# Three chains in PSUM for layer 1's up units, and eight copies behind the last square

## The chip, the cores and the metric

The kernel runs on one core of one Trainium2 chip. The metric is the device time of one execution in microseconds. Five engines work side by side: TensorE (PE) multiplies matrices into the eight banks of PSUM; VectorE (DVE), ScalarE (ACT) and GpSimd (POOL) work elementwise; SyncE (SP) issues DMA transfers. Each engine runs its own instructions in order and waits for the others through semaphores.

## What is computed

A decoder trunk of two layers over 512 tokens of width 1024: layer 0 is a convolution module and a SwiGLU FFN, layer 1 is windowed attention and a SwiGLU FFN, with a final norm. The change lies in the FFN of layer 1, where attention has just been added to h:

```python
def rmsnorm(x, g):
    xf = xf * lax.rsqrt(jnp.mean(xf * xf, axis=-1, keepdims=True) + EPS)
    return xf * g

def swiglu_ffn(x, w_up, w_down):
    gate, up = jnp.split(x @ w_up, 2, axis=-1)
    return (jax.nn.silu(gate) * up) @ w_down

h = h + attn @ w_o[j]
h = h + swiglu_ffn(rmsnorm(h, norm_ffn[l]), ffn_w_up[l], ffn_w_down[l])
return rmsnorm(h, norm_final)
```

The hidden width is 2816.

## The kernel before

**Split products.** All weights and activations in this part are fp32 split into a high and a low part, and each product is three matmuls: high x high, high x low, low x high (`mm3`, lines 356 to 358). Weights come in chunks of 128 x 1024 from DRAM (`load`, line 248, SP's queue, into four buffers). `split_weights` makes the high part on ACT (a cast, line 273) and the low part on DVE (line 276); both have four buffers, and the split runs three chunks ahead of PE.

**The up product in pairs.** The 2816 hidden columns are worked in eleven pairs (0 to 10) of 256 gate and 256 up columns. Pairs 0, 2, 4, 7 and 10 are plain (`plain_pair`): 96 matmuls of 512 columns in four banks. The pairs in `SEVENS` (1, 3, 5, 6, 8, 9), here called units, use a scheme of seven block products in place of eight (`seven_pair`): the weights are cut into A11, A12, A21, A22, the activations into B11 to B22, and besides plain blocks there are sums S1 to S4 of weight blocks and T1 to T4 of activation blocks. A block is 24 matmuls of 256 columns into one bank. The S sums are made beforehand by DMAs that add in DRAM (`prepare`, lines 264 and 268, on SP's and POOL's queues).

Before the change every block of a unit has a bank of its own, seven a unit. The elementwise engines put the results together in four gate tiles c11 to c22: ACT copies A11 (line 787) and S1 (789); when S2 is done DVE adds it to c11 (791) and combines it with S3 (792), POOL adds and subtracts (793, 794); A12, S4 and A22 are added or subtracted by DVE (796, 798, 800). The order of the blocks in a unit is A11, S3, S1, S2, A12, S4, A22, and in unit 1 A11, S1, S3, S2, A12, S4, A22. Afterwards the gate is scaled (806, DVE), passed through silu (807, ACT) and multiplied (808, POOL), and `forms_of` makes the T sums of the result (822, POOL) and splits them (lines 515 to 519, ACT and DVE) for the down product.

**The down product** (`low_pairs`, line 848) takes two pairs at a time, also in seven blocks, in the order A11, S1, S2, A12, S3, S4, A22, and adds several blocks up in PSUM in three chains x, y, z, two banks each, given by `CHAINS` (chain, and where the result goes):

```python
    CHAINS = {"A11": ("x", 0, 0), "S1": ("z", 1, 1), "S2": ("x", 0, 1), "A12": ("y", 0, 0), "S3": ("x", 1, 1),
              "S4": ("z", 0, 1), "A22": ("x", 1, 0)}
```

DVE reads a chain after each block (857); A12 goes through ACT and POOL (854, 855). The order of the stages is up 0, 1, 2, low 0, then up p, up p+1, low p-1 for p = 3, 5, 7, 9.

**The seam.** Attention's output product ends with eight tiles of h, one after another. For each tile DVE adds it to h (line 1410), and `Rows.on_h` makes the scaled high part on ACT (`split_scaled`, line 510) and the low part on DVE (511), squares the tile on ACT (463) and adds the squares on DVE (467). Their sum goes through eight one-column products (477), a power on POOL (481) and a product (503) to the scale of the rows. `Rows.sums` makes the activation's T blocks for the units: eight copies of h scaled by the gain on ACT (726), four subtractions or additions on POOL (732), then splits (515 to 519). It is stepped from inside pair 0. In unit 1, between blocks, PE also transposes h by four products (`flip`, 1425) and ACT copies the result (1426).

**Order.** The program is written in one order, but a planner with its own time estimates puts each engine's instructions in the order in which they are issued: a ready instruction is taken before one that would wait. PSUM banks come from a pool of eight. `tc.issue_after(x)` forces an instruction behind x on x's engine.

Of the kernel before, what the change touches and what calls it, by code (L numbers as in the profile page):

```python
# [14 lines left out]
ALU = mybir.AluOpType  # L15
# [37 lines left out]

SEVEN = ("A11 B11", "S3 T3", "S1 T1", "S2 T2", "A12 B21", "S4 B22", "A22 T4")
SEVENS = (1, 3, 5, 6, 8, 9)
SEVEN_FIRST = ("A11 B11", "S1 T1", "S3 T3", "S2 T2", "A12 B21", "S4 B22", "A22 T4")
SEVEN_LOW = ("A11 B11", "S1 T1", "S2 T2", "A12 B21", "S3 T3", "S4 B22", "A22 T4")


def by_seven(layer, pair):
    return layer == 1 and pair in SEVENS


def order_of(kind, pair):
    if kind == "low":
        return SEVEN_LOW
    return SEVEN_FIRST if pair == SEVENS[0] else SEVEN


def ups(layer, pair):
# [4 lines left out]


def blocks_of(kind, pair):
    return [(kind, pair, n.split()[0]) for n in order_of(kind, pair)]  # L80


def is_block(c):
# [3 lines left out]
def chunk_plan():  # L87
# [28 lines left out]
    for kind, pair in STEPS1:  # L116
        plan.extend(blocks_of(kind, pair) if kind == "low" or by_seven(1, pair) else ups(1, pair))
# [82 lines left out]
def hybrid_trunk(ctx: ExitStack, tc: tile.TileContext, xT, W, prm_in, wdw_in, sinks, relb, onehot, fin, lead, out):  # L200
    nc = tc.nc
# [10 lines left out]
    def uid(s):  # L212
        ctr[0] += 1
        return f"{s}{ctr[0]}"

    def bank():
        return ps.tile([P, 512], F32, tag="bank", name=uid("bank"))

    def quad(dt=F32R):
        return quads.tile([P, 4, 512], dt, tag="quad", name=uid("quad"))  # L220

    def temp():
        return tmp.tile([P, 512], F32, tag="tmp", name=uid("tmp"))
# [69 lines left out]
    def get_seven(kind, pair, n):  # L293

        advance()
        u = stream["use"]
        stream["use"] += 1
        assert PLAN[u] == blocks_of(kind, pair)[n]
        return splits.pop(u)
# [49 lines left out]
        sh = dict(a=n)  # L349
        return tuple(w and w.rearrange("p (a b) -> p a b", **sh) for w in (hi, lo))  # L350

    def mm3(out, w, x, start, stop):
        if w[1] is None:
            nc.tensor.matmul(out, w[0], x, start=start, stop=stop)  # L354
            return
        nc.tensor.matmul(out, w[0], x[0], start=start, stop=False)  # L356
        nc.tensor.matmul(out, w[0], x[1], start=False, stop=False)  # L357
        nc.tensor.matmul(out, w[1], x[0], start=False, stop=stop)  # L358

    class Act:  # L360
        def __init__(self, n, w=512):
# [33 lines left out]
    h = [hT[:, i, :] for i in range(KT)]  # L395
# [53 lines left out]
    def col(name, i):  # L449
        c = PARAM_COLS[name] + i  # L450
        return prm[:, c:c + 1]


    class Rms:
# [5 lines left out]

        def add(self, t):
            sq = temp()[:, 0:self.w]
            nc.scalar.square(sq, t)  # L463
            if self.acc is None:
                self.acc = sq
            else:
                self.eng.tensor_add(sq, self.acc, sq)  # L467
                self.acc = sq
# [44 lines left out]
    def split(dst, src, negative=False):  # L513
        if negative:
            nc.scalar.mul(dst[0], src, -1.0)
            nc.vector.scalar_tensor_tensor(dst[1], src, -1.0, f32(dst[0]), op0=ALU.mult, op1=ALU.subtract)
            return
        nc.scalar.copy(dst[0], src)
        nc.vector.tensor_sub(dst[1], src, f32(dst[0]))
# [190 lines left out]
    class Rows:  # L710
# [12 lines left out]
        def sums(self):  # L723
            f = [quad(F32) for _ in range(2)]
            for i in range(KT):
                nc.scalar.mul(f[i // 4][:, i % 4, :], h[i], col(self.gain, i))
            b11, b12, b21, b22 = (x[:, :, s] for x in f for s in HALF)
            t1 = self.pool.tile([P, 1024], F32, tag="sum", name=uid("t1"), bufs=1).rearrange("p (k s) -> p k s", k=4)

            for name, t, f, a, b in (("T1", t1, nc.gpsimd.tensor_sub, b11, b12), ("T3", b12, nc.gpsimd.tensor_sub, b22, b12),  # L730
                                     ("T2", b11, nc.gpsimd.tensor_add, b12, b11), ("T4", b21, nc.gpsimd.tensor_sub, b11, b21)):
                f(t, a, b)
                yield
                both = quads.tile([P, 2, 4, 256], F32R, tag="quad", name=uid("rows"))
                self.block[name] = [both[:, a] for a in range(2)]
                split(self.block[name], t, name == "T2")

    def new_gates(pool):
        return pool.tile([P, 2, 2, 2, 256], F32, tag="up", name=uid("up"), bufs=3)
# [32 lines left out]
    def seven_pair(pair, rows, pool, between=None):  # L772

        c = new_gates(pool)
        c11, c12, c21, c22 = (c[:, m, s] for m in range(2) for s in range(2))
        acc = {}
        for n, name in enumerate(order_of("up", pair)):
            w = [x.rearrange("p (a k c) -> p a k c", a=2, k=4) for x in get_seven("up", pair, n)]
            a, b = name.split()
            x = rows.block[b]  # L780
            r = acc[a] = bank().rearrange("p (a s) -> p a s", a=2)
            for which in range(2):
                for k in range(4):
                    mm3(r[:, which], [v[:, which, k, :] for v in w], [x[e][:, k, :] for e in range(2)],
                        which == 0 and k == 0, which == 1 and k == 3)
            if a == "A11":
                nc.scalar.copy(c11, r)
            elif a == "S1":
                nc.scalar.copy(c22, r)
            elif a == "S2":  # L790
                nc.vector.tensor_add(c12, r, c11)
                nc.vector.scalar_tensor_tensor(c21, acc["S3"], -1.0, c12, op0=ALU.mult, op1=ALU.subtract)
                nc.gpsimd.tensor_add(c12, c12, c22)
                nc.gpsimd.tensor_sub(c22, c21, c22)
            elif a == "A12":
                nc.vector.tensor_add(c11, r, c11)
            elif a == "S4":
                nc.vector.tensor_add(c12, r, c12)
            elif a == "A22":
                nc.vector.tensor_sub(c21, c21, r)  # L800
            if between is not None:
                between()
        rs_bc = rows.rms.step2().rearrange("p (s q) -> p s q", s=2)
        for m in range(2):
            gate = c[:, m, :, 0, :]
            nc.vector.tensor_mul(gate, gate, rs_bc)
            nc.scalar.activation(gate, gate, AF.Silu)
            nc.gpsimd.tensor_mul(gate, gate, c[:, m, :, 1, :])
        return c
# [3 lines left out]
    def forms_of(c, pool, odd):  # L813
# [9 lines left out]
        for part in (slice(0, 2), slice(3, 4), slice(4, 8)):  # L823
# [3 lines left out]
    CHAINS = {"A11": ("x", 0, 0), "S1": ("z", 1, 1), "S2": ("x", 0, 1), "A12": ("y", 0, 0), "S3": ("x", 1, 1),  # L827
              "S4": ("z", 0, 1), "A22": ("x", 1, 0)}

    def rows_of(g, t):  # L830
        return hT[:, g * 4:(g + 1) * 4, t * P:(t + 1) * P]

    def low_pairs(pair, forms, rs):

        chains = {}
        for n, name in enumerate(order_of("low", pair)):
            whi, wlo = get_seven("low", pair, n)
            a, b = name.split()
            chain, g, s = CHAINS[a]
            first = chain not in chains  # L840
            if first:
                chains[chain] = [bank() for _ in range(2)]
            for t, out in enumerate(chains[chain]):
                for e in range(2):
                    xh, xl = (f[:, FORM[b], t * P:(t + 1) * P] for f in forms[e])
                    ws = slice(e * 512, (e + 1) * 512)
                    for i, (x, w) in enumerate(((xh, whi), (xh, wlo), (xl, whi))):
                        nc.tensor.matmul(out, x, w[:, ws], start=first and e == 0 and i == 0, stop=e == 1 and i == 2,  # L848
                                         skip_group_check=True)
                to, scale = rows_of(g, 2 * s + t), (rs[1] if g else rs[0])[:, 2 * s + t:2 * s + t + 1]  # L850
                src = out.rearrange("p (i c) -> p i c", i=4)
                if a == "A12":
                    m = temp()
                    nc.scalar.mul(m, out, scale)
                    nc.gpsimd.tensor_add(to, to, m.rearrange("p (i c) -> p i c", i=4))
                else:
                    nc.vector.scalar_tensor_tensor(to, src, scale, to, op0=ALU.mult, op1=ALU.add)
# [22 lines left out]
    with tc.tile_pool(name="conv", bufs=2) as cv:  # L880
# [234 lines left out]
        first = [Pw1(0, 0, raw, turn=True)]  # L1115
# [104 lines left out]
    if True:  # L1220
        ffn_part(0, 1, x0["ffn0"], ALL, Both(), nxt.on_h)
        x, rms = nxt.x, nxt.rms
# [31 lines left out]
        for n in range(4):  # L1254
            nc.vector.tensor_scalar(vq[:, n].rearrange("p a g c -> p (a g c)"), vb[n][:, 0:256], rs[:, n:n + 1], None,
                                    op0=ALU.mult)
# [126 lines left out]
        for part in range(2):  # L1383
            for g in range(2):
# [23 lines left out]
                for m in range(4):  # L1408
                    i = g * 4 + m
# [42 lines left out]
    for b in range(NBLK):  # L1452
# [3 lines left out]
        for g, (whi, wlo) in enumerate(whole):  # L1456
            acc = bank()
# [50 lines left out]
```

## Time and profile before

| | |
|---|---|
| median of 3 runs | 1071.57 us (1064.79 to 1073.39) |
| the profiled execution's own time | 1072.48 us |
| its span in the trace | 1070.1 us |
| mean granted clock of TensorE | 0.994 |

A profile is of one execution. The span runs from the first to the last instruction; the rest of the execution's time lies around it. Rows of a timeline give start, duration, engine, line, operation, what is written and read, and how many instructions were merged; in brackets stands the engine's idle time just before and what ended it. The chain of work that ended last is followed back from the last instruction, so its shares say which engine set the time. Rows of windows give, for a stretch, PE, PE's weight loads, DVE, ACT and POOL as busy us with their instruction count, then granted clock, DMA share and GB/s.

### The profile page before, as it was taken

The numbers are of one execution on the slowest core, as the hardware profiler recorded it, in microseconds if no ns is written. First come the engines' busy times: TensorE is split into PE (matmuls) and PEld (weight loads), VectorE is DVE, ScalarE is ACT, GpSimd is POOL, SyncE is SP. The second block draws the span as 40 slices with busy tenths as digits, with TensorE's granted clock in tenths as the row PEclk, the third lists the DMA queues.
The fourth block names the chain that finished last, engine by engine and source line by source line (L and its number), as shares of the span: only waits on it lengthen the run. The fifth ranks groups of instructions, "written<-read, shape, count | busy, mean of one in ns | idle before, by whom it ended". The sixth has DMA issues, their size and how long they took to land.

```text
span 1070.1 us, 16002 instructions
## 1 busy us (share of the span) xinstructions
PE 1054.9 (99%) x5878; PEld 917.0 (86%) x5878; DVE 748.5 (70%) x1159; ACT 554.1 (52%) x968; POOL 432.8 (40%) x523
## 2 busy tenths in 40 slices
PE   9999999999999999999999999998999999999996
PEld 7888889999988888888888877777989899898985
DVE  3999988977777644444436466487767778768867
ACT  3887888755565333222343565474544355444543
POOL 3999998710321312211212344123532415315401
PEclk9999999999999999999999999998999999999998
DMA  9238046565556777676766444455989655545532
GB/s 356 86 98 98 3 141 214 178 230 184 177 183 191 236 203 211 169 211 190 189 188 188 138 109 137 118 158 158 277 229 332 213 188 179 157 156 177 180 118 79
DMA packets 52059, 187.92 MB, mean 176 GB/s; under 512 B 6188, under 2 KB 12493, under 8 KB 51277
## 3 DMA queue, kind: packets, MB, share of 16 engines
q1 hardware_dynamic: 44924, 162.74, 46.4%
q0 software_dynamic: 6336, 23.07, 12.6%
q8 instruction: 46, 0.75, 0.3%
q10 hardware_dynamic: 720, 1.10, 0.3%
q14 instruction: 33, 0.26, 0.1%
HBM read 181.64 MB, written 51.38 MB: 218 GB/s over the span
## 4 chain that ended last, share of the span: by engine, by line
PE 96%; DVE 2%; ACT 1%; issue 1%; DMA 1%; POOL 0%; SPq 0%
PE bank L356 19%; PE bank L357 19%; PE bank L358 19%; PE bank L906 10%; PE bank L848 9%; PE bank L388 5%; PE bank L354 4%; PE bank L389 3%; PE bank L1304 1%; PE bank L1346 1%; PE bank L1333 1%; PE bank L1004 1%; DMA both<-in_lead_dram 1%; PE bank L894 1%; PE bank L1461 0%
## 5 line engine op out<-in xcount | busy, mean ns | idle before, releaser
L276 DVE TENSOR_TENSOR wlo<-raw,whi 128x1024 fp32r<-128x1024 f32 x219 | 299.7, 1371 | 175.2 <-ACT whi L273 174.1
L273 ACT CAST whi<-raw 128x1024 fp32r<-128x1024 f32 x219 | 229.6, 1049 | 311.7 <-PE bank L357 199.7
L357 PE MATMUL bank<-quad,whi 128*128 128x512 f32 (+1 forms) x1008 | 349.8, 347 | 3.9 <-DVE quad L511 3.9
L356 PE MATMUL bank<-quad,whi 128*128 128x512 f32 (+1 forms) x1008 | 350.1, 348 | 0.0
L358 PE MATMUL bank<-quad,wlo 128*128 128x512 f32 (+1 forms) x1008 | 349.4, 347 | 0.0
L357 PEld LDWEIGHTS bank<-quad,whi 128*128 128x128 f32 x1008 | 191.5, 190 | 27.5 <-DVE quad L511 4.3
L356 PEld LDWEIGHTS bank<-quad,whi 128*128 128x128 f32 x1008 | 191.6, 190 | 24.8 <-issue 1.6
L358 PEld LDWEIGHTS bank<-quad,wlo 128*128 128x128 f32 x1008 | 191.5, 190 | 23.9 <-issue 0.6
L948 POOL TENSOR_TENSOR pr<-pr,pr 128x256 f32<-128x256 f32 x208 | 156.9, 812 | 6.6 <-ACT pr L947 6.6
L955 DVE SCALAR_TENSOR_TENSOR bank<-apad,wdw,bank 128x256 f32<-128x256 f32 x248 | 112.4, 484 | 3.4
L947 ACT ACTIVATE pr<-apad,wdw 128x256 f32<-128x256 f32 x208 | 98.2, 501 | 14.8 <-POOL pr L948 13.0
L906 PE MATMUL bank<-quad,w 128*128 128x256 f32 x448 | 98.7, 380 | 0.0
L906 PEld LDWEIGHTS bank<-quad,w 128*128 128x128 f32 x448 | 84.9, 190 | 11.8 <-DVE bank L955 0.2
L388 PE MATMUL bank<-quad,whi 128*128 128x512 f32 x212 | 75.9, 398 | 0.0
L268 POOL DMA_DIRECT2D sum<-in_W_dram x22 | 18.3, 833 | 123.0 <-DMA sum<-in_W_dram 122.8
L822 POOL TENSOR_TENSOR up<-up 128x256 f32<-128x256 f32 x40 | 44.2, 1114 | 43.0 <-DVE up L768 41.4
L268 POOL DMA_DIRECT2D sum<-sum x22 | 18.0, 818 | 105.8 <-DMA sum<-in_W_dram 104.3
L389 PE MATMUL bank<-quad,wlo 128*128 128x256 f32 x212 | 59.3, 280 | 0.0
L467 POOL TENSOR_TENSOR tmp<-tmp,tmp 128x256 f32<-128x256 f32 (+1 forms) x28 | 27.0, 963 | 79.1 <-ACT tmp L463 62.8
L848 PE MATMUL bank<-wlo,fhi 128*128 128x512 f32 x140 | 55.1, 393 | 0.0
L356 PE MATMUL bank<-rows,whi 128*128 128x256 f32 x192 | 54.6, 285 | 0.0
L358 PE MATMUL bank<-rows,wlo 128*128 128x256 f32 x192 | 54.3, 283 | 0.0
(220 smaller groups left out, 1603.3 us busy)
## 6 DMA issues: line engine op xcount, KB each, us to landing
raw<-in_W_dram SPq DMA_DIRECT2D x187, 512.0 KB, 3.8
sum<-in_W_dram SPq DMA_DIRECT2D x44, 512.0 KB, 5.4
raw<-sum SPq DMA_DIRECT2D x44, 512.0 KB, 3.9
sum<-in_W_dram POOLq DMA_DIRECT2D x22, 512.0 KB, 6.6
sum<-sum POOLq DMA_DIRECT2D x22, 512.0 KB, 6.4
w<-in_W_dram SPq DMA_DIRECT2D x14, 512.0 KB, 9.0
fd<-fs SPq DMA_DIRECT2D x1, 3072.0 KB, 34.1
h<-in_xT_dram SPq DMA_DIRECT2D x8, 256.0 KB, 8.4
```

The lines of the kernel that those rows point to most:

```text
L273: on_act = nc.scalar.copy(hi, src).ins
L276: latest[:] = [on_act, lo_engine[0].tensor_sub(lo, src, f32(hi)).ins]
L356: nc.tensor.matmul(out, w[0], x[0], start=start, stop=False)
L357: nc.tensor.matmul(out, w[0], x[1], start=False, stop=False)
L358: nc.tensor.matmul(out, w[1], x[0], start=False, stop=stop)
L388: nc.tensor.matmul(first[2], first[0], first[1], start=start, stop=False)
L389: nc.tensor.matmul(second[2], second[0], second[1], start=False, stop=stop)
L848: nc.tensor.matmul(out, x, w[:, ws], start=first and e == 0 and i == 0, stop=e == 1 and i == 2, skip_group_check=True)
L906: mm = nc.tensor.matmul(self.pb[:, w * W2:(w + 1) * W2], w1_of(ct, w, k), x[k] if x else xg[k][:, tok], start=k == 0, stop=k == KT - 1)
L947: on_act = nc.scalar.mul(pr, a[:, j:j + W2], tap(j))
L948: on_pool = nc.gpsimd.tensor_add(pr, acc, pr)
L955: on_dve = nc.vector.scalar_tensor_tensor(yt if i == nd - 1 else c, src, tap(i), c if i else self.shift, op0=ALU.mult, op1=ALU.add)
```

## The change

The units take the order A11, S1, S2, A12, S3, S4, A22 and the three chains of the down product, one bank each. A block is added in PSUM to what its chain already holds, so the bank is read and then written further: ACT copies x after A11 (c11) and after S2 (c12), takes z negated after S1 (c22) and x negated after A22 (c21); DVE subtracts x from c22 after S3 and adds y to c11 after A12 and z to c12 after S4. POOL does nothing there any more. The three orders become one. T2 is made from B22 and T1 instead of from B11 and T3, and the order of the T blocks is T1, T2, T3, T4.

At the seam, the eight scaled copies of h are forced behind the last square on ACT.

```diff
-SEVEN = ("A11 B11", "S3 T3", "S1 T1", "S2 T2", "A12 B21", "S4 B22", "A22 T4")
+SEVEN = ("A11 B11", "S1 T1", "S2 T2", "A12 B21", "S3 T3", "S4 B22", "A22 T4")
...
-            nc.scalar.square(sq, t)
+            self.squared = nc.scalar.square(sq, t).ins
...
-                nc.scalar.mul(f[i // 4][:, i % 4, :], h[i], col(self.gain, i))
+                with tc.issue_after(self.rms.squared):
+                    nc.scalar.mul(f[i // 4][:, i % 4, :], h[i], col(self.gain, i))
...
-            for name, t, f, a, b in (("T1", t1, nc.gpsimd.tensor_sub, b11, b12), ("T3", b12, nc.gpsimd.tensor_sub, b22, b12),
-                                     ("T2", b11, nc.gpsimd.tensor_add, b12, b11), ("T4", b21, nc.gpsimd.tensor_sub, b11, b21)):
+            for name, t, f, a, b in (("T1", t1, nc.gpsimd.tensor_sub, b11, b12), ("T2", b11, nc.gpsimd.tensor_add, b22, t1),
+                                     ("T3", b12, nc.gpsimd.tensor_sub, b22, b12), ("T4", b21, nc.gpsimd.tensor_sub, b11, b21)):
...
-            x = rows.block[b]
-            r = acc[a] = bank().rearrange("p (a s) -> p a s", a=2)
+            x, chain = rows.block[b], CHAINS[a][0]
+            first = chain not in chains
+            if first:
+                chains[chain] = bank().rearrange("p (a s) -> p a s", a=2)
+            r = chains[chain]
             for which in range(2):
                 for k in range(4):
                     mm3(r[:, which], [v[:, which, k, :] for v in w], [x[e][:, k, :] for e in range(2)],
-                        which == 0 and k == 0, which == 1 and k == 3)
+                        first and which == 0 and k == 0, which == 1 and k == 3, skip_group_check=True)
             if a == "A11":
                 nc.scalar.copy(c11, r)
             elif a == "S1":
-                nc.scalar.copy(c22, r)
+                nc.scalar.mul(c22, r, -1.0)
             elif a == "S2":
-                nc.vector.tensor_add(c12, r, c11)
-                nc.vector.scalar_tensor_tensor(c21, acc["S3"], -1.0, c12, op0=ALU.mult, op1=ALU.subtract)
-                nc.gpsimd.tensor_add(c12, c12, c22)
-                nc.gpsimd.tensor_sub(c22, c21, c22)
+                nc.scalar.copy(c12, r)
             elif a == "A12":
                 nc.vector.tensor_add(c11, r, c11)
+            elif a == "S3":
+                nc.vector.tensor_sub(c22, c22, r)
             elif a == "S4":
                 nc.vector.tensor_add(c12, r, c12)
             elif a == "A22":
-                nc.vector.tensor_sub(c21, c21, r)
+                nc.scalar.mul(c21, r, -1.0)
```

More of the change, by code (lines that the diff above doesn't have):

```diff
@@ L51 @@
 NPARAM = _c
-SEVEN = ("A11 B11", "S3 T3", "S1 T1", "S2 T2", "A12 B21", "S4 B22", "A22 T4")
+SEVEN = ("A11 B11", "S1 T1", "S2 T2", "A12 B21", "S3 T3", "S4 B22", "A22 T4")
 SEVENS = (1, 3, 5, 6, 8, 9)
-SEVEN_FIRST = ("A11 B11", "S1 T1", "S3 T3", "S2 T2", "A12 B21", "S4 B22", "A22 T4")
-SEVEN_LOW = ("A11 B11", "S1 T1", "S2 T2", "A12 B21", "S3 T3", "S4 B22", "A22 T4")
 def by_seven(layer, pair):
     return layer == 1 and pair in SEVENS
[L66 to L69, printed above, removed]
 def ups(layer, pair):
@@ L79, in blocks_of @@
 def blocks_of(kind, pair):
-    return [(kind, pair, n.split()[0]) for n in order_of(kind, pair)]
+    return [(kind, pair, n.split()[0]) for n in SEVEN]
 def is_block(c):
@@ L350, in get, with mm3 @@
         return tuple(w and w.rearrange("p (a b) -> p a b", **sh) for w in (hi, lo))
-    def mm3(out, w, x, start, stop):
+    def mm3(out, w, x, start, stop, **kw):
         if w[1] is None:
@@ L355, in mm3 @@
             return
-        nc.tensor.matmul(out, w[0], x[0], start=start, stop=False)
-        nc.tensor.matmul(out, w[0], x[1], start=False, stop=False)
-        nc.tensor.matmul(out, w[1], x[0], start=False, stop=stop)
+        nc.tensor.matmul(out, w[0], x[0], start=start, stop=False, **kw)
+        nc.tensor.matmul(out, w[0], x[1], start=False, stop=False, **kw)
+        nc.tensor.matmul(out, w[1], x[0], start=False, stop=stop, **kw)
     class Act:
@@ L775, in seven_pair @@
         c11, c12, c21, c22 = (c[:, m, s] for m in range(2) for s in range(2))
-        acc = {}
-        for n, name in enumerate(order_of("up", pair)):
+        chains = {}
+        for n, name in enumerate(SEVEN):
             w = [x.rearrange("p (a k c) -> p a k c", a=2, k=4) for x in get_seven("up", pair, n)]
             a, b = name.split()
-            x = rows.block[b]
-            r = acc[a] = bank().rearrange("p (a s) -> p a s", a=2)
+            x, chain = rows.block[b], CHAINS[a][0]
[3 more added lines that the diff above has]
+            r = chains[chain]
             for which in range(2):
@@ L835, in low_pairs @@
         chains = {}
-        for n, name in enumerate(order_of("low", pair)):
+        for n, name in enumerate(SEVEN):
             whi, wlo = get_seven("low", pair, n)
```

## The prediction

> **What bounds the kernel now.** I read the page first (busy time, then the chain that ended last), then the waits of TensorE, then engine by engine the timeline around the one long wait they name, and last the stages of layer 1's up units.
>
> ```profile
> span 1070.1 us, 16002 instructions
> PE 1054.9 (99%) x5878; PEld 917.0 (86%) x5878; DVE 748.5 (70%) x1159; ACT 554.1 (52%) x968; POOL 432.8 (40%) x523
> PE 96%; DVE 2%; ACT 1%; issue 1%; DMA 1%; POOL 0%; SPq 0%
> PE bank L357 <- DVE quad L511: 3.9, 1, 3.9
> PE bank L894 <- DVE quad L868: 1.2, 1, 1.2
> PE bank L441 <- POOL ones_m L438: 1.1, 1, 1.1
> ```
>
> TensorE (PE) is busy 99% and is 96% of the chain. Its whole list of waits has three entries, and two of them lie at the start of the program. So no matmul block of layer 1's up units waits for anything today, and neither do the down products of L848, which already run in three chains. What the change takes from VectorE and GpSimd cannot shorten a stage in which only PE sets the pace. The one place where time can come back is the 3.9 us wait, and it lies at the seam between attention and layer 1's FFN, which the second edit touches. What PE did there (start, duration, and in brackets the idle time before and its releaser; an x8 row is eight merged instructions):
>
> ```profile
> 720.59 0.61 PE L356 MATMUL bank<-quad,whi 128*128 128x512 f32 x2
> 725.08 0.50 PE L357 MATMUL bank<-quad,whi 128*128 128x512 f32 x1 [3.88 <-DVE quad L511]
> 725.90 0.57 PE L358 MATMUL bank<-quad,wlo 128*128 128x512 f32 x1
> 726.26 1.70 PE L477 MATMUL bank<-ones_c,tmp 128*128 128x1 f32 x8
> 727.82 0.77 PE L356 MATMUL bank<-quad,whi 128*128 128x512 f32 x1
> ...
> 732.96 0.40 PE L356 MATMUL bank<-quad,whi 128*128 128x512 f32 x1
> 733.19 0.40 PE L357 MATMUL bank<-quad,whi 128*128 128x512 f32 x1
> 568.53 0.79 PE bank L477 x8
> 720.00:730.00 10.00, 6.12 (x23) 4.95 (x22) 9.90 (x8) 3.94 (x5) 6.16 (x3) 0.80 0.23 74
> 730.00:740.00 10.00, 10.00 (x39) 8.05 (x39) 6.79 (x6) 2.01 (x2) 3.56 (x3) 0.86 0.79 200
> ```
>
> The seam costs more than its 3.88 us. At full pace two matmuls of 512 columns start 0.23 us apart (732.96 to 733.19). Without a wait the next one would have started at 720.59 + 2 x 0.23 = 721.05. From there to 733.19 lie 17 matmuls (four from 725.08 to 725.90, thirteen from 727.82 to 732.96) and the eight one-column products of L477, which took 0.79 us elsewhere (the row at 568.53, from the chain). That is 17 x 0.23 + 0.79 = 4.70 us of work, so PE would have been at 725.75: the seam loses 733.19 - 725.75 = 7.44 us. About 4.0 is the wait, and 3.4 a slow clock behind it: the granted clock (third number from the end) is 0.80 and 0.86 in the two windows, and 1.00 in the stages quoted further down.
>
> A rule of the Trainium skill (TensorE: Matmul & The Clock Gate, Part 1) says that the clock falls to half after an idle window of about 3.4 us and returns after one busy window of that length. By one such window an estimate of the slow-clock loss would be 1.7 us and the gain 5.7; the rows show twice that loss, and I go by the rows.
>
> **The seam edit.** The late operand is the low part of the last tile of h (L511). Its history, on ACT, DVE and POOL:
>
> ```profile
> 709.73 0.71 ACT L510 ACTIVATE quad<-h,prm 128x512 fp32r<-128x512 f32 x1
> 710.87 3.78 ACT L726 ACTIVATE quad<-h,prm 128x512 f32<-128x512 f32 x6
> 717.25 0.71 ACT L510 ACTIVATE quad<-h,prm 128x512 fp32r<-128x512 f32 x1
> 717.87 0.62 ACT L463 ACTIVATE tmp<-h 128x512 f32<-128x512 f32 x1
> 711.87 0.68 DVE L1410 TENSOR_TENSOR h<-bank,h 128x512 f32<-128x512 f32 x1
> 718.74 0.74 DVE L511 SCALAR_TENSOR_TENSOR quad<-h,prm,quad 128x512 fp32r<-128x512 f32 x1
> 722.21 2.82 DVE L511 SCALAR_TENSOR_TENSOR quad<-h,prm,quad 128x512 fp32r<-128x512 f32 x1
> 721.81 2.67 POOL L732 TENSOR_TENSOR quad<-quad 128x1024 f32<-128x1024 f32 x1
> 728.24 1.97 POOL L481 TENSOR_TENSOR rs<-ms,mhalf 128x4 f32<-128x4 f32 x1 [3.76 <-DVE ms L479]
> 745.24 0.37 PE L356 MATMUL bank<-rows,whi 128*128 128x256 f32 x1
> ```
>
> The last h tile is ready at 711.87 + 0.68 = 712.55, but ACT starts its scaled high part at 717.25: it is running eight scaled copies (L726, 3.78 / 6 = 0.63 us each). These in turn let POOL start the T subtractions (L732), and while those run a DVE operation of 0.74 us takes 2.82. The edit sends all eight copies behind the last square. Then ACT does high part and square at 712.6 to 713.9 (0.71 + 0.62), DVE the low part by 714.7, or by about 716 with a weight split in front. PE wants it at 721.05: five microseconds of room, so both wait and slow clock go: -7.44 us.
>
> What is late next? The eight copies now end at 714 + 8 x 0.63 = 719, 720 with a weight cast (1.05) between. POOL's four T operations, 2.67 each, start after the first four copies at about 717.5 and end by 728; with the 1.97 of L481 between them, 730. The rows' splits lag by some 2 us each. PE first reads rows of T1 at 745.24, after the change at about 737.8; T2 is wanted one block (2.88, below) and one flip later, T3 and T4 after that. T1 stands at about 722 and T2 at 725, so more than ten microseconds are left. The DVE operations that POOL stretches are then weight splits, each of which serves 24 matmuls (5.5 us); DVE can be stretched to 2.8 on each and keep up. This new work at 717 to 730 costs nothing under that cover; without it, a T1 row late by x costs x.
>
> **The chains, six units.** Per unit DVE loses the add and the combination at S2 and the subtraction at A22 and gains one at S3; POOL loses two operations; ACT gains two copies (S2, A22; that of S1 gets a factor).
>
> ```profile
> L787 ACT COPY up<-bank x6: 564/580/582, 746.8 to 990.3; 128x512 f32<-128x512 f32 x6
> L792 DVE SCALAR_TENSOR_TENSOR up<-bank,up x6: 691/691/692, 756.0 to 1001.3; 128x512 f32<-128x512 f32 x6
> L793 POOL TENSOR_TENSOR up<-up x6: 2135/2144/2146, 756.8 to 1002.2; 128x512 f32<-128x512 f32 x6
> 868.30:888.20 19.90, 19.90 (x157) 19.37 (x157) 16.12 (x17) 10.53 (x14) 3.79 (x3) 1.00 0.59 185
> 888.20:908.40 20.20, 20.20 (x170) 20.20 (x169) 17.93 (x18) 11.21 (x15) 12.72 (x9) 1.00 0.56 186
> SPq L248 <- DVE wlo L276: 114.3, 37, 8.3
> ```
>
> DVE: 2 x 0.69 x 6 = 8.3 us less; POOL: over 6 x 2.14 = 12.8 less; ACT: 2 x 0.58 x 6 = 7.0 more. The two windows are units 5 and 6: PE fills them whole, ACT is busy 10.5 and 11.2 of 20 us. All three sums are beside the path: zero. The matmuls stay the same in number and shape. S3's weights are used later, those of S1 and S2 one block earlier; the loads of layer 1 wait for free buffers behind DVE's splits (last row, 114 us), not for the sums they fetch: zero.
>
> New are the turns. PE may not write chain x again before it has been read: S2 waits for ACT's copy of A11, S3 for ACT's copy of S2, A22 for DVE's subtraction of S3. That is three turns a unit, 18 in all, each with one block of matmuls as cover. A turn holds up PE, and with it every block and down product queued behind. The trace has no such wait, so I bound it from ACT's and DVE's reads after a block today:
>
> ```profile
> 876.61 1.05 ACT L273 CAST whi<-raw 128x1024 fp32r<-128x1024 f32 x1 [1.83 <-PE bank L357]
> 877.57 0.58 ACT L789 COPY up<-bank 128x512 f32<-128x512 f32 x1
> 879.49 1.06 ACT L273 CAST whi<-raw 128x1024 fp32r<-128x1024 f32 x1 [1.35 <-PE bank L357]
> 879.62 0.69 DVE L791 TENSOR_TENSOR up<-bank,up 128x512 f32<-128x512 f32 x1 [0.70 <-PE bank L358]
> 895.64 0.42 ACT L515 ACTIVATE fhi<-up 128x256 fp32r<-128x256 f32 x1 [3.02 <-POOL up L822]
> ...
> 898.79 0.58 ACT L789 COPY up<-bank 128x512 f32<-128x512 f32 x1
> 899.65 1.05 ACT L273 CAST whi<-raw 128x1024 fp32r<-128x1024 f32 x1 [0.29 <-PE bank L357]
> ```
>
> A cast that waits for PE starts as a block ends, so a block is 879.49 - 876.61 = 2.88 us. In unit 5 the block ends at 876.61, the cast goes first, and the copy is done at 878.15: 1.54 us of 2.88. DVE reads (879.62) within 0.13 us of the block's end and is done 0.7 later. Such turns cost nothing. In unit 6 ACT has stood 3.02 us for POOL. The block before the one that ended at 899.65 ended at 896.77, and its copy at 899.37: 2.60 of 2.88, and this third place in the unit will be S2's. A22 now goes through ACT behind a cast (1.54) where DVE took 0.8; unit 5's POOL work, for which ACT stands here, starts about 0.75 later, and 0.75 - 0.28 = 0.47 us of PE is lost. Ends for all turns: 0, and 12 ACT turns as bad as a full POOL stand with a split of 1.05 and the copy behind it (3.02 + 1.05 + 0.58 - 2.88 = 1.8 us each), 21 us. A gain is excluded, since no bank is waited for today. I take 0.5, since most units look like unit 5.
>
> Sum: 1072.48 (the profiled execution; 1070.1 is its span, 2.4 lie around it) - 7.44 + 0.5 = 1065.5. The median shown is 0.91 below that execution, which gives 1064.6; I say 1065.
>
> **Rivals.** (1) Turns become the bound: ACT works in order, and a copy stands behind casts, silu and splits that wait for POOL. Against it: unit 5 and DVE's prompt reads, and no wait at L848. For it: unit 6, and the flips in unit 1, which give ACT another 0.58 a block. From a mean of 7.44 / 18 = 0.4 us a turn the seam's gain is gone, from 1.0 us the kernel is 1% slower; the bad end is 1064.1 + 21 = 1085.
>
> (2) The gap at the seam only shrinks: DVE's weight splits come in front of the low part, or the statistics products of L477 find the last sum late. A wait of up to 3.5 us might stay without the slow clock: 1064.6 + 3.5 = 1068.
>
> (3) The edit does not do what it says at the seam, because the last tile waits for DVE, not for the copies: 1071.57 + 0.5 = 1072. Against it: ACT's eight copies sit between 710.87 and the high part.
>
> A page bears on (2). The Trainium skill (SBUF — State Buffer, Who interferes with whom) says that a DVE operation with two SBUF inputs is blocked for the whole of a GpSimd operation that reads SBUF. The trace agrees: 0.74 against 2.82 us for L511.
>
> **How the numbers follow.** The forecast has 0.64, rival 1 0.16, rival 2 0.12, rival 3 0.08. A measurement of this kernel tells about 1% (10.7 us) from no change; the three runs lie 0.8% apart. The forecast is 0.6% faster, so I give 0.16 of its 0.64 to over 1%: that takes 3.9 us beyond the seam, about half that spread. Of rival 1, 0.10 lies beyond 1% slower. Faster 0.16, same 0.74, slower 0.10. Range: down 6 us from the forecast by the spread of the runs (1059), up through rivals 2 and 3 and the milder half of rival 1 (1076).
>
> **What would show it.** At the seam: L726 behind the last L463 on ACT, L511 at its 0.74 us, no PE wait there, granted clock 1.00 in the windows from 720 to 740, unit 1 some 7.4 us earlier. In the units: at most one short PE wait on ACT's copy of S2 in unit 6; the up and down stages as long as before. I am wrong if PE's waits list ACT or DVE reads of chain x with several microseconds in sum, if L511 still ends a wait at the seam, or if the time moved somewhere else, as in the last 20 us.

## The result, and the profile after

The changed kernel takes 1065.32 us (median of 20 runs, 1063.86 to 1067.74) against 1070.95 us before (20 runs, 1064.79 to 1073.39) on the same chip. The ratio is 0.9956, 95% interval 0.9944 to 0.9968: 0.4% faster, clear of the noise, and close to the 1065 of the forecast.

The page of the changed kernel and its list of TensorE's waits (waiting line, releaser, us in total, times, longest). The lines of the file have moved up by nine, further down by eight, so L357 is now L348, L511 is L502, L726 is L718, L732 is L724:

```profile
span 1065.8 us, 15971 instructions
PE 1052.5 (99%) x5878; PEld 914.7 (86%) x5878; DVE 728.6 (68%) x1147; ACT 559.6 (53%) x980; POOL 406.9 (38%) x511
...
PE bank L494 <- ACT tmp L480: 1.4, 1, 1.4
PE bank L432 <- POOL ones_m L429: 1.1, 1, 1.1
PE bank L888 <- DVE quad L862: 0.9, 2, 0.6
PE bank L345 <- ACT plain L689: 0.8, 1, 0.8
PE bank L347 <- ACT up L786: 0.2, 1, 0.2
```

DVE has 20 us less work and POOL 26 less, while the median fell by 5.6; e2 below shows that this relief lies beside the path. The wait at the seam is gone. The last entry is a turn, of 0.2 us. The other two new entries, 1.4 and 0.8 us, lie in layer 0, where nothing was changed (at about 184 and 168 us).

To see where the time went, compare when the n-th matmul starts in the two traces (5878 in each; TensorE's order ahead of the seam is the same in both). Worked out from the traces:

| matmul | what runs there | before, us | after, us | difference |
|---|---|---|---|---|
| 600 | layer 0, convolution | 132.63 | 132.41 | -0.22 |
| 1000 | layer 0, behind the convolution | 198.78 | 201.40 | +2.62 |
| 3800 | last of attention's output product | 692.92 | 695.54 | +2.62 |
| 4000 | unit 1 | 743.69 | 738.92 | -4.76 |
| 4200 | behind unit 1 | 768.84 | 764.55 | -4.29 |
| 5877 | last matmul | 1060.72 | 1056.42 | -4.30 |

Three steps: +2.84 in layer 0, -7.38 at the seam, +0.47 in unit 1; then both run alike for 290 us, with five more units in them. The seam in the changed kernel, by ACT, DVE and POOL, and the two windows (this trace is 2.62 us behind that of before when it comes to the seam):

```profile
715.75 0.71 ACT L501 ACTIVATE quad<-h,prm 128x512 fp32r<-128x512 f32 x1
716.36 0.62 ACT L454 ACTIVATE tmp<-h 128x512 f32<-128x512 f32 x1
716.89 5.02 ACT L718 ACTIVATE quad<-h,prm 128x512 f32<-128x512 f32 x8
718.09 0.74 DVE L502 SCALAR_TENSOR_TENSOR quad<-h,prm,quad 128x512 fp32r<-128x512 f32 x1
722.88 2.69 DVE L267 TENSOR_TENSOR wlo<-raw,whi 128x1024 fp32r<-128x1024 f32 x1 [3.45 <-ACT whi L264]
719.59 2.41 POOL L724 TENSOR_TENSOR t<-quad 128x1024 f32<-128x1024 f32 x1 [2.05 <-ACT quad L718]
720.00:730.00 10.00, 10.00 (x49) 8.39 (x48) 7.12 (x4) 6.86 (x9) 9.92 (x4) 1.00 0.52 153
730.00:740.00 10.00, 10.00 (x54) 8.38 (x54) 9.87 (x10) 5.56 (x6) 4.02 (x3) 1.00 0.55 124
```

The eight copies stand behind the last square; the last tile's low part takes 0.74 us; POOL's first T operation starts after it. What POOL now stretches is a weight split (2.69 us). PE is busy throughout at granted clock 1.00, where before it had 0.80 and 0.86.

The +2.84 in layer 0 is no part of the change. DVE and POOL there, first in the trace after, then in the one before:

```profile
161.37 4.59 DVE L502 SCALAR_TENSOR_TENSOR quad<-h,prm,quad 128x256 fp32r<-128x256 f32 x1
159.46 6.22 POOL L942 TENSOR_TENSOR pr<-pr,pr 128x256 f32<-128x256 f32 x9
```

```profile
161.59 0.48 DVE L511 SCALAR_TENSOR_TENSOR quad<-h,prm,quad 128x256 fp32r<-128x256 f32 x1
159.69 11.42 POOL L948 TENSOR_TENSOR pr<-pr,pr 128x256 f32<-128x256 f32 x13
```

The same DVE operation took 0.48 us in one execution and 4.59 in the other, in which it ended only when POOL's run of additions was over (six of the nine in the row lie beside it). Before, both engines moved on together, and POOL took 0.9 us an addition instead of 0.7.

### The profile page after: what moved, and what is told of

Read it like the earlier page. It is cut to its first block, busy times and chain, and to the rows that moved or that the text cites. A ratio compares the mean times of both kernels' runs of the same rounds, so it can differ in the third digit from the quotient of the medians.

```text
span 1065.8 us, 15971 instructions
## 1 busy us (share of the span) xinstructions
PE 1052.5 (99%) x5878; PEld 914.7 (86%) x5878; DVE 728.6 (68%) x1147; ACT 559.6 (53%) x980; POOL 406.9 (38%) x511
## 4 chain that ended last, share of the span: by engine, by line
PE 91%; DVE 3%; ACT 3%; DMA 1%; issue 1%; POOL 1%; SPq 0%; DVEq 0%; POOLq 0%
PE bank L347 20%; PE bank L349 20%; PE bank L348 20%; PE bank L842 9%; PE bank L900 8%; PE bank L379 5%; PE bank L380 3%; PE bank L1298 1%; PE bank L1340 1%; PE bank L1327 1%; ACT pr L941 1%; DVE bank L949 1%; PE bank L998 1%; DVE quad L502 1%; DMA both<-in_lead_dram 1%
## 5 line engine op out<-in xcount | busy, mean ns | idle before, releaser
L267 DVE TENSOR_TENSOR wlo<-raw,whi 128x1024 fp32r<-128x1024 f32 x219 | 293.0, 1341 | 189.8 <-ACT whi L264 189.0
L348 PE MATMUL bank<-quad,whi 128*128 128x512 f32 (+1 forms) x1008 | 348.7, 346 | 0.0
L348 PEld LDWEIGHTS bank<-quad,whi 128*128 128x128 f32 x1008 | 191.0, 189 | 23.1 <-issue 0.2
L802 POOL TENSOR_TENSOR up<-up 128x512 f32<-128x512 f32 x12 | 20.1, 1672 | 94.3 <-ACT up L801 94.3
L842 PE MATMUL bank<-whi,flo 128*128 128x512 f32 x140 | 54.5, 393 | 0.0
```

Source lines behind the costliest of these rows:

```text
L267: latest[:] = [on_act, lo_engine[0].tensor_sub(lo, src, f32(hi)).ins]
L348: nc.tensor.matmul(out, w[0], x[1], start=False, stop=False, **kw)
```

## The experiments

**Each edit alone, and the changed kernel once more.** e1 adds the seam edit to the kernel before; e2 takes it out of the changed kernel; e3 is the changed kernel.

```diff
# e2, against the changed kernel (e1: the same lines the other way in the kernel before, with the line that keeps the last square)
-                with tc.issue_after(self.rms.squared):
-                    nc.scalar.mul(f[i // 4][:, i % 4, :], h[i], col(self.gain, i))
+                nc.scalar.mul(f[i // 4][:, i % 4, :], h[i], col(self.gain, i))
```

> The kernel before with the seam edit alone (seven banks a unit, the old orders). Theory: the whole gain is the seam, so no wait of TensorE behind L511 and granted clock 1.00 there, unit 1 about 7.4 us earlier against the same point ahead of the seam; time 0.3 to 0.7% below before, and equal to the changed kernel or up to 0.5 us faster, since it has no turns. Rival (the chains carry part of the gain, through DVE and GpSimd relieved): less than half of it, above 1068 us.

> The changed kernel without the seam edit (chains, eight copies free to go ahead of the last squares). Theory: the wait behind L511 of about 3.9 us and the slow clock come back, and the chains cost 0 to 0.5 us: same as before within 1 us, 1070 to 1072 us. Rival (chains give a gain of their own): 1066 to 1069 us.

> The changed kernel once more, for a second trace. Ahead of the seam its trace was 2.6 us late against that of before, though the instructions there stand in the same order: one DVE operation (split of a scaled tile, 0.48 us) took 4.59 us while GpSimd ran six additions back to back. Theory: this is chance of one execution, so the second trace may have it or not, and the times spread by some 3 us; rival: it is fixed to this kernel, then it stands in every trace of it and in none of before.

| kernel | median us (range, runs) | ratio to before, 95% |
|---|---|---|
| before, same chip | 1071.47 (1065.64 to 1074.0, 17) | |
| e1, seam edit alone | 1065.57 (1064.77 to 1065.71, 5) | 0.9944 (0.9925 to 0.9964) |
| e2, chains alone | 1070.65 (1066.31 to 1076.01, 12) | 1.0002 (0.9983 to 1.0021) |
| e3, the changed kernel | 1065.02 (1064.84 to 1065.65, 5) | 0.9942 (0.9922 to 0.9962) |

All of the gain is the seam's, and the chains alone give none that the runs can tell (the interval of e2 is 0.2% to either side), as the theory had it. In e1's trace the difference to before is -0.20 us ahead of the seam and -7.59 from unit 1 to the end, without a step at any unit. e3's is -0.05, then -7.44, then -6.89 from unit 1's end on: the turns cost 0.55 us in the trace. The medians of e1 and e3 differ by as much, the other way, so the runs do not resolve it.

e3 has no stall in layer 0: the operation that took 4.59 us takes 0.49, with all instructions in the same order as in the first trace of this kernel.

```profile
161.31 0.49 DVE L502 SCALAR_TENSOR_TENSOR quad<-h,prm,quad 128x256 fp32r<-128x256 f32 x1
```

None of the later traces has it either. So it is not fixed to the kernel; how often an execution has it was not counted.

e2's waits, its seam and its granted clock, and in the last row the clock in the trace of before:

```profile
PE bank L468 <- DVE tmp L458: 1.6, 1, 1.6
PE bank L348 <- DVE quad L502: 1.2, 1, 1.2
...
721.50:722.66 1.16, 0.00 (x1) 0.00 (x0) 1.16 (x2) 0.00 (x0) 1.16 (x2) 1.00 0.00 0
722.66:723.86 1.20, 1.20 (x4) 0.67 (x4) 1.20 (x1) 0.15 (x1) 1.20 (x1) 1.00 0.00 0
723.86:725.45 1.59, 0.00 (x2) 0.01 (x1) 1.59 (x2) 1.59 (x2) 1.59 (x2) 1.00 0.00 0
...
727.00:729.00 2.00, 2.00 (x7) 1.57 (x6) 2.00 (x2) 1.04 (x1) 0.62 (x1) 0.54 0.00 0
729.00:731.00 2.00, 2.00 (x7) 1.54 (x6) 2.00 (x4) 0.00 (x0) 1.01 (x1) 0.61 0.13 20
...
726.00:732.70 6.70, 6.70 (x22) 5.54 (x21) 6.60 (x6) 2.95 (x3) 4.42 (x2) 0.50 0.52 181
```

The seam's wait is back, this time in two pieces of 1.16 and 1.59 us with 1.2 us of matmuls between. The clock halves all the same: 0.54 and 0.61 over two microseconds each make about 3.4 us at half speed. In the trace of before it was 0.50 from about 726 to 732.7, twice as long. So e2's trace loses only 4.9 us at the seam against e1's and e3's, not 7.4. The loss also differs between runs of one kernel: the mean granted clock of the 17 runs of before lies between 0.992 and 0.998, that of all runs of e1 and e3 is 0.997 or 0.998. The clock is not the whole of the spread, though: the six runs of before at 0.997 or 0.998 took 1065.64 to 1073.15 us, and where the rest comes from stays open.

**What at the seam makes the last tile late.** The copies do two things: they take ACT's time, and they let POOL begin the T operations early, which stretch DVE's. e4 lets all eight copies go early again and holds only POOL, by a small copy that reads the last square's buffer and so comes behind DVE's addition of that square, which follows the last low part. e7 holds only the last four copies.

```diff
# e4, against e2
+            self.sq = sq
...
+            mark = small.tile([P, 4], F32, tag="mark", name=uid("mark"))
+            held = [nc.gpsimd.tensor_copy(mark, self.rms.sq[:, 0:4]).ins]
...
-                f(t, a, b)
+                with tc.issue_after(held[0]):
+                    held[0] = f(t, a, b).ins
# e7, against the changed kernel
-                with tc.issue_after(self.rms.squared):
+                with tc.issue_after(self.rms.squared) if i >= 4 else nullcontext():
```

> As e2, the eight copies again ahead of the last squares on ACT, but GpSimd's T operations are held until the last square exists. Theory A: at the seam the copies alone do not make the last tile late; the lock does, with which GpSimd's T operations stretch DVE's L511 from 0.74 to 2.8 us. Then the wait of TensorE is gone here too, L511 of the last tile starts at about 718 us on the clock of before, and the time is that of the changed kernel, 1064 to 1067 us. Theory B: ACT's time for the copies is the cause, then a wait of 2 to 4 us stays and the time is 1068 to 1072 us.

> The changed kernel, but only the last four scaled copies are held behind the last square; the first four may go as early as before, so GpSimd's first T operation can start early, while the second must wait. Theory (ACT's time for the copies is not what costs, the lock on the last tile's L511 is): no wait of TensorE at the seam, granted clock 1.00, time as the changed kernel within 1 us. Rival (every copy ahead of the last high part costs): half of the seam's loss comes back, 2 to 4 us.

e4: 1065.13 us (1063.09 to 1065.78, 6 runs), ratio 0.9937 (0.9917 to 0.9958): the whole gain, with all eight copies early. e7: 1070.99 us (1069.32 to 1072.36, 10 runs; before, measured with e5 to e8, 1071.94), ratio 0.9993 (0.998 to 1.0005): no gain, with the last four late. ACT, DVE, POOL of e4, at the last tile:

```profile
717.54 0.72 ACT L502 ACTIVATE quad<-h,prm 128x512 fp32r<-128x512 f32 x1
718.33 0.74 DVE L503 SCALAR_TENSOR_TENSOR quad<-h,prm,quad 128x512 fp32r<-128x512 f32 x1
719.92 2.39 POOL L728 TENSOR_TENSOR t<-quad 128x1024 f32<-128x1024 f32 x1
```

and the same of e7, with the weight split ahead on DVE and the wait of PE:

```profile
714.96 0.71 ACT L501 ACTIVATE quad<-h,prm 128x512 fp32r<-128x512 f32 x1
713.93 3.91 DVE L267 TENSOR_TENSOR wlo<-raw,whi 128x1024 fp32r<-128x1024 f32 x1 [1.25 <-ACT whi L264]
719.04 2.88 DVE L502 SCALAR_TENSOR_TENSOR quad<-h,prm,quad 128x512 fp32r<-128x512 f32 x1
714.07 2.69 POOL L724 TENSOR_TENSOR t<-quad 128x1024 f32<-128x1024 f32 x1
718.79 2.57 POOL L724 TENSOR_TENSOR quad<-quad,t 128x1024 f32<-128x1024 f32 x1 [2.04 <-ACT quad L718]
721.97 0.50 PE L348 MATMUL bank<-quad,whi 128*128 128x512 f32 x1 [1.24 <-DVE quad L502]
```

In e4 ACT is as late with the high part as before (717.54), and no harm follows: DVE does the low part in 0.74 us before POOL starts. TensorE's instructions stand in the same order in e4 and e2, and so do ACT's and DVE's up to the last low part, so POOL's start is what differs. In e7 ACT is done with the high part at 715.67, about 1 us before e4 begins it when both are set against before's clock (e7 runs 0.46 us ahead of it, e4 0.29 behind), and PE waits nevertheless. POOL's first T operation, free as soon as four copies are there, stretches the weight split to 3.91 us (1.23 in e4); that pushes the low part to 719.04, into the second T operation, which stretches it to 2.88. So the expectation of e7 was wrong in its result and right in its cause: what POOL does to DVE decides, and it also works through what DVE has queued ahead.

**What a turn costs.** e5 and e6 put two and three more copies of the same bank on ACT ahead of the copy at A11's and S2's turn; the results stay the same.

```diff
# e6 (e5: range(2)), against the changed kernel
...
+            if a in ("A11", "S2"):
+                for _ in range(3):
+                    slow = nc.scalar.copy(junk.rearrange("p (a s) -> p a s", a=2), r).ins
+                turn = tc.issue_after(slow)
...
-                nc.scalar.copy(c12, r)
+                with turn:
+                    nc.scalar.copy(c12, r)
```

> The changed kernel with two more copies of the same bank on ACT ahead of each copy at the turns A11 and S2 (12 turns, 0.58 us each, so 1.16 us more per turn; the results are the same). Theory: a turn has 2.88 us of cover and uses 1.54 in the common case, so 2.70 still fits; only unit 1, where a turn is already short by 0.2 to 0.3 us, pays about 1.2. Time 1 to 3 us over the changed kernel. Rival (turns are not covered by the next block but by chance): 12 x 1.16, 14 us over it.

> As e5 with three more copies (1.74 us more per turn): 1.54 + 1.74 = 3.28 is 0.4 us over the cover, so most of 12 turns pay 0.4 and unit 1 about 1.8: 5 to 8 us over the changed kernel. Rival: the planner puts other blocks of matmuls in between, and the sum stays below 3 us.

e5: 1066.26 us (1064.49 to 1066.64, 5 runs), ratio to before 0.9948 (0.9928 to 0.9968). That is 1.2 over e3, but the ranges overlap, and before stood 0.5 higher here than with e3. In the traces e5 loses 0.97 us from unit 1 to the end and e3 0.55. e6: 1071.24 us (1069.24 to 1073.44, 10 runs), 6.2 over e3, ratio to before 0.9997 (0.9985 to 1.001). Both sizes are as expected, but for e6 that is luck, since its waits of PE are not what the theory had named:

```profile
PE bank L349 <- DVE wlo L267: 1.6, 2, 1.3
...
PE bank L851 <- DVE wlo L267: 0.9, 2, 0.5
PE bank L851 <- ACT whi L264: 0.7, 1, 0.7
PE bank L347 <- ACT up L792: 0.6, 1, 0.6
```

Only the last row is a turn (0.6 us, in unit 1). The other 3.2 us are weights that come late: ACT's queue is longer, the casts stand behind it, and PE waits for the split parts. The bad end of a turn is thus, in this run, ACT's queue as a whole and not the chain's bank.

Nor do the two runs say how much delay one block hides, because the planner did what the rival of e6 had named and put other blocks in between. Counted in the traces, in unit 1 of the changed kernel 2 matmuls of A12 stand ahead of S2; in e5 there are 20, and in e6 all 24 and four of S4. What a turn hides when the order is kept stays open.

**The one turn that waits.**

```diff
# e8, against the changed kernel
-                nc.scalar.copy(c12, r)
+                nc.vector.tensor_copy(c12, r)
```

> The changed kernel with DVE in place of ACT for the copy of x after S2. Theory: the one turn at which TensorE still waits (unit 1, S2 to S3, 0.2 to 0.3 us) is ACT's queue; DVE reads a bank within 0.15 us of a block's end, so no wait at any turn is left, and the time is 0 to 0.6 us below the changed kernel, which the times cannot show. Rival: DVE stands behind a stretched weight split there and the wait only changes its name.

e8: 1066.53 us (1065.0 to 1067.12, 5 runs), ratio 0.9963 (0.9938 to 0.9988), no better than the changed kernel. The rival was right that the wait only changes its name. What DVE's copy stood behind was a split of the gated result, not a stretched weight split (in the trace 748.87 + 1.22, then the copy at 750.02):

```profile
PE bank L347 <- DVE up L786: 0.2, 1, 0.2
```

## Why the prediction was right

**The seam, 7.44 us.** Right in size. From matmul 3800 to 4000 the changed kernel gained 7.38 us, e1 7.39 and e3 7.39. The medians show less, 5.6 to 6.5 us. The trace of before is one execution (1072.48 us) on the slow side of its runs, and the slow clock, nearly half of the sum, comes out differently in each. Taking the sum against that execution and then moving by the median's 0.91 gave 1064.6 where 1065.32 was measured. That the number came out so close is partly luck: the forecast is 6.6 us below the 1071.57 known then, the measured gain is 5.6, and the median of before came out 0.6 lower in 20 runs than in three.

**Its cause.** The prediction named both parts, ACT's eight copies and POOL's T operations that the copies set free, but gave its time line to the first: high part at 712.6 in place of 717.25. e4 and e7 show that ACT's delay alone costs nothing and that POOL's early start brings the loss back even when ACT is in time (all of it in e7's median, 5.0 of 7.4 us in its trace, which has the slow clock once). The edit works since POOL cannot begin before the copies. Rival 3, that the last tile waits for DVE, was right about the engine and wrong about the outcome.

**What is late next.** Nothing, as predicted, though with less room. T1's rows were put at about 722 and T2's at 725; DVE finished those splits at 725.50 + 3.42 and 728.91 + 3.34, which is 726.3 and 729.6 on before's clock, since POOL and DVE stretch each other (such a split took 1.21 us in the trace of before):

```profile
725.50 3.42 DVE L510 TENSOR_TENSOR rows<-t,rows 128x1024 fp32r<-128x1024 f32 x1
728.91 3.34 DVE L507 SCALAR_TENSOR_TENSOR rows<-quad,rows 128x1024 fp32r<-128x1024 f32 x1
740.48 0.37 PE L347 MATMUL bank<-rows,whi 128*128 128x256 f32 x1
```

PE reads T1's rows first at 740.48, so more than eleven microseconds were left.

**The turns, 0.5 us.** Right in sum (0.47 and 0.55 us in the two traces), wrong in place. It was put in unit 6, behind the splits that wait for POOL, and it came in unit 1. ACT of the changed kernel there, and PE at the turn:

```profile
747.98 1.06 ACT L1420 COPY h<-bank 128x512 f32<-128x512 f32 x2
...
749.24 1.05 ACT L509 CAST fhi<-up 128x1024 fp32r<-128x1024 f32 x1
750.18 1.07 ACT L264 CAST whi<-raw 128x1024 fp32r<-128x1024 f32 x1
751.13 0.60 ACT L786 COPY up<-bank 128x512 f32<-128x512 f32 x1
751.78 0.38 PE L347 MATMUL bank<-rows,whi 128*128 128x256 f32 x1 [0.20 <-ACT up L786]
```

The copy of S2 stands behind a split and a cast, and these behind two copies of a flip; the prediction had this queue, by the flips, as a point for rival 1. In unit 6 the copy of S2 is done at 896.50 + 0.58 = 897.08, and PE begins S3 at 898.18, so 1.1 us were left where the prediction had none:

```profile
893.78 0.42 ACT L506 ACTIVATE fhi<-up 128x256 fp32r<-128x256 f32 x1 [2.62 <-POOL up L816]
...
896.50 0.58 ACT L786 COPY up<-bank 128x512 f32<-128x512 f32 x1
893.86 0.28 PE L347 MATMUL bank<-quad,whi 128*128 128x256 f32 x1
898.18 0.28 PE L347 MATMUL bank<-rows,whi 128*128 128x256 f32 x1
```

The step that failed is the cover. The prediction took one block of 24 matmuls, 2.88 us, between S2 and S3. The planner put 36 there, of A12 and S4 (they read `quad`, the blocks of sums read `rows`): 36 x 0.12 = 4.3 us from 893.86 to 898.18. With 24, S3 would have come at 896.74, ahead of the copy's end, and the 0.5 us might have fallen where it was put. ACT also stood 2.62 us for POOL in place of 3.02. So the sum of the turns is right in size by luck.

**Relief of DVE and POOL: zero.** e2 shows it: chains alone, 1.0002 of before (0.9983 to 1.0021).

**The clock.** The rows gave 3.4 us of loss and the prediction went by them. By the Trainium skill (TensorE: Matmul & The Clock Gate, Part 1), where the clock is full again after at least one busy window of about 3.4 us, it had estimated one such window at half speed. The trace of before had two such stretches, and e2 and e7 had one, so the length agrees. What sets their number three traces do not say: one wait of 3.88 us came with two, the two shorter waits of e2 and of e7 with one.

## What to carry to other kernels

Where an engine ends the wait of the bottleneck, ask not only what delayed its input but what stretched its own operation: here a DVE operation that took four times its usual time pointed at POOL, and holding POOL back for a few microseconds gave the whole gain with nothing moved on ACT (e4). A wait in a matmul stream can cost more than its length: 4.0 us of wait came with 3.4 us of slow clock in one trace, and the waits of e2 with half of that. With the wait closed the runs lie closer together as well (20 runs over 8.6 us before, 3.9 after). Adding up in PSUM was nearly free here, 0.5 us for 18 turns, with other matmuls between a block and the next on its chain and room in the reader's queue; with three more copies at each of 12 turns the weights behind that queue came late.

## What the runs showed of the hardware that was not expected

With identical instructions in identical order, one DVE operation with two SBUF inputs took 4.59 us in one execution and 0.48 in another, and PE ended up 2.84 us later. It ended with POOL's run of additions of 0.7 us each, six of which lie beside it, as if it had waited for the end of the run and not just of the operation in progress; this was seen once. The Trainium skill (SBUF — State Buffer, Who interferes with whom) tells of an exclusive lock that is held for one whole instruction; that the waiting engine may be passed over several times is how this one execution reads, and nothing here tests it.

Two waits of TensorE, of 1.16 and 1.59 us with 1.20 us of full work between, came ahead of a halved granted clock (e2), though neither is half as long as the 3.88 us in the trace of before. e7 repeats it: waits of 1.24 and 1.59 us, and a clock of 0.51 and 0.64 from 726 to 728 and 728 to 730.
